# A recurrent scan on one core: first products of a chain step issued a step ahead, and small reduction products issued a step behind their operands

## The chip, the cores and the metric

One core of a Trainium2 chip runs the whole program. The metric is device time in microseconds (us). The tensor engine is called PE here, the vector engine DVE, the scalar engine ACT, GpSimd POOL, and the engine that issues most transfers SP.

## What is computed

The program is a small network over 512 latent tokens and 256 context tokens of width 1024. The change touches its first mixer alone, a linear recurrence with a 64 by 64 state per head, 16 heads, run in two directions (`wkv7_scan`), the coefficient of its bonus term, and the norm of its keys:

```python
kk = to_heads(k * k_k.astype(f32), RK_HEADS, RK_HEAD)
kk = kk / jnp.maximum(jnp.sqrt(jnp.sum(kk * kk, axis=-1, keepdims=True)), 1e-12)
...
s_kk = jnp.einsum('bhvk,bhk->bhv', s, kk_t)
s = (s * w_t[:, :, None, :] - s_kk[..., None] * (kk_t * a_t)[:, :, None, :]
     + v_t[..., None] * k_t[:, :, None, :])
return s, jnp.einsum('bhvk,bhk->bhv', s, r_t)
...
coef = jnp.einsum('bthn,zbthn,hn->bth', r, k_dir, r_k.astype(jnp.float32))
bonus = (coef[..., None] * v).reshape(b, n, D_MODEL)
```

The index z of `coef` runs over the two directions, so `coef` sums over both.

## The kernel before

The recurrence is done in chunks of 64 tokens, 12 chunks in each direction. A pair f of heads (f = 0 to 7) goes through three chains of four steps, `chain(f, 0)` to `chain(f, 2)`; the first is over the context, the other two over the latent tokens. Both directions and both heads of the pair go through a step together. A step (L844 to L896) is:

1. POOL scales the old state S (L850, tile SP). PE multiplies the values, UV, with the masked Gram matrix GA, and adds the product of S with KR to it, in place 0 of the PSUM tile `ch` (L856 and L859; for latent chunks also products into `y`, L861). ACT copies the sum out as Rs (L863). `ch` is one tile with one buffer, taken anew in each step, so the first product of a step waits until everything of the step before has been read.
2. PE multiplies Rs with the inverse TF into place 1 (L868), and ACT writes the result back into UV (L871).
3. PE multiplies UV with BT into place 2 (L877) and with GA into `y` (L881). DVE makes the new S from place 2 and SP (L890; L888 in the first step).
4. S becomes the old state of the next step; nothing is issued here.

`mm` (L831) issues all products of the chain, so the trace has them at L833; `mm` keeps the last of them in `last`. After each of the four parts the chain yields. `weave` (L991) then runs `fill` and the sides in turn. `fill` (L1030) takes as many pieces of the background work as PACE allots to this slot, 384 slots in all, and `tc.issue_after` places what they put on PE behind the last product of the chain. The background work is `job` (L954): the key, receptance and value projections of later pairs (products at L979), and behind them a conditioning product (`ada`, L235). The sides are pieces of the inversion of the next chunks (`inv`, L765: products at L790 and L795, ACT copies T at L797, DVE transposes at L799, DVE masks at L792), the Gram products (`gram`, L716, products at L739) and the features of the next pair (`feats1`, `feats2`); a side is not placed behind the chain. The order within an engine is set by a planner from the order of the code and its own estimate of when an operand is ready.

`feats2` (L667) makes, for each of the two directions in turn, the scaled keys `bk` (L693 to L701; DVE does one half of the partitions, POOL the other), and then the bonus coefficient: DVE multiplies receptance, `r_k` and this direction's keys (z, L704; the trace names the tile t), PE sums it over the head's 64 partitions with four products of two columns (L707, each in two passes, so eight records), and ACT copies the result (L709) or, for the second direction, DVE adds it (L711).

`k_out` (L327) takes a finished key projection: for each of two feature blocks ACT copies it out of PSUM (L334), SP stores it (L335), ACT squares it (L337), and PE sums the squares by products of two columns (L340). Copies and squares share the tag `st`, two buffers in the scan. `k_norm` (L343) has POOL raise the sums to the power -1/2 and PE transpose them (L348).

Of the kernel before, what the change touches and what calls it, by code (L numbers as in the profile page):

```python
# [12 lines left out]
OP = mybir.AluOpType  # L13
# [18 lines left out]
PACE = ((-13, 0), (0, 13), (28, 25), (60, 33), (76, 49), (124, 73), (140, 89), (156, 97), (172, 113),  # L32
        (220, 137), (236, 153), (252, 161), (268, 177), (384, 217))
# [271 lines left out]
def phase_rwkv(k, tables, tables2, modulate, yg):  # L305
# [18 lines left out]
    W = {"r": a["rk_w_rkv"][0, 0], "k": a["rk_w_rkv"][0, 1], "v": a["rk_w_rkv"][0, 2]}  # L324
    halves = lambda ps: ps.rearrange("p (i n) -> p i n", i=2)

    def k_out(p, pss, lat, pool, tag, psp, pt):  # L327

        c0, c1 = (0, NT) if lat else (NT, NA)
        pn = k.t(psp, [128, 512], tag=pt)[:, :24]  # L330
        for i, ps in enumerate(pss if lat else [halves(pss[0])[:, i] for i in range(2)]):
            f = 2 * p + i
            t = k.t(pool, [128, 512], tag=tag)[:, :c1 - c0]
            nc.scalar.copy(out=t, in_=ps)  # L334
            nc.sync.dma_start(out=kd_[f][:, c0:c1], in_=t)  # L335
            sq = k.t(pool, [128, 512], tag=tag)[:, :c1 - c0]
            nc.scalar.activation(out=sq, in_=ps, func=AF.Square, scale=k.v1["k_k"][:, f:f + 1])  # L337
            for b in range((c1 - c0) // 128):
                o = c0 // 32 + 4 * b + 2 * i
                nc.tensor.matmul(pn[:, o:o + 2], sq[:, b * 128:(b + 1) * 128], k.c["blk2"], start=True, stop=True)  # L340
        nc.vector.tensor_scalar(out=rq[:, c0 // 32:c1 // 32], in0=pn[:, c0 // 32:c1 // 32], scalar1=1e-24, scalar2=None, op0=OP.max)

    def k_norm(p, psp, pt):  # L343
        nc.gpsimd.tensor_tensor(out=rq, in0=rq, in1=k.mhalf.to_broadcast([128, 24]), op=OP.pow)
        for b0, b1 in ((0, 4), (4, 6)):
            ps = k.t(psp, [128, 512], tag=pt)
            for b in range(b0, b1):
                nc.tensor.transpose(ps[:4, (b - b0) * 128:(b - b0 + 1) * 128], rq[:, 4 * b:4 * b + 4], k.ident)  # L348
            hi = rn[heads(p), b0 * 128:b1 * 128]
            nc.scalar.copy(out=hi, in_=ps[:4, :(b1 - b0) * 128])  # L350
            q = 64 * (p % 2) + 32
            nc.vector.tensor_tensor(out=rn[q:q + 4, b0 * 128:b1 * 128], in0=ps[:4, :(b1 - b0) * 128], in1=hi.bitcast(F32), op=OP.subtract)

    def r_out(p, pss, lat, pool, tag, *_):
        for i, ps in enumerate(pss):
            t = k.t(pool, [128, 512], tag=tag)
            nc.scalar.copy(out=t, in_=ps)
            nc.sync.dma_start(out=rd_[2 * p + i], in_=t)

    def v_out(p, pss, lat, pool, tag, *_):  # L360
        for i, ps in enumerate(pss):
            t = k.t(pool, [128, 512], tag=tag)
            nc.vector.tensor_copy(t, ps)
            b = 2 * i if lat else 4
            nc.sync.dma_start(out=vd[b * 128:(b + 2) * 128, p * 256:(p + 1) * 256].rearrange("(b p) n -> p b n", p=128), in_=halves(t))
    OUT = {"k": k_out, "r": r_out, "v": v_out}


    with ExitStack() as ea:
# [124 lines left out]
        k_out(0, ks, True, sp3, "st", psn, "mm")  # L494
        k_out(0, [kc], False, sp3, "st", psn, "mm")
        k_norm(0, psn, "mm")
# [14 lines left out]
        for p in range(2):  # L511
            r_out(p, rs[2 * p:2 * p + 2], True, sp3, "st")
# [12 lines left out]
        v_out(0, vs[:2], True, sp3, "st")  # L525
        v_out(0, vs[2:], False, sp3, "st")


    with ExitStack() as eb:
# [137 lines left out]
        def feats2(f):  # L667
# [21 lines left out]
            for d in range(2):  # L689
# [13 lines left out]
                z = k.t(fp2, [128, NA], tag="t1")[:, :NT]  # L703
                nc.vector.scalar_tensor_tensor(out=z, in0=rT, scalar=V["r_k"][:, f:f + 1], in1=kd[:, 0:NT], op0=OP.mult, op1=OP.mult)  # L704
                ps = k.t(psf, [128, 512], tag="gm")
                for b in range(4):
                    nc.tensor.matmul(ps[:, 2 * b:2 * b + 2], z[:, b * 128:(b + 1) * 128], k.c["blk2"], start=True, stop=True)  # L707
                if d == 0:
                    nc.scalar.copy(out=cf, in_=ps[:, 0:8])  # L709
                else:  # L710
                    nc.vector.tensor_tensor(out=cf, in0=cf, in1=ps[:, 0:8], op=OP.add)  # L711
                yield
            st.update(KR=KR, BK=BK, PC=PC)
# [120 lines left out]

        def chain(f, bt):
# [8 lines left out]
            for s4 in range(4):  # L844
# [18 lines left out]
                nc.scalar.copy(out=Rs, in_=pc_[:, 0])  # L863
                yield
                for d in range(2):
                    for par in range(2):
                        q = PR(1 - par)
                        mm(pc_[q, 1, d, :], TF[q, s4, d, :], Rs[q, d, :], start=True, stop=True, skip_group_check=True)  # L868
                for par in range(2):
                    q = PR(1 - par)  # L870
                    nc.scalar.activation(out=UV[q, par, s4], in_=pc_[q, 1], func=AF.Copy, scale=-1.0)  # L871
                yield
                for d in range(2):
                    for par in range(2):
                        q = PR(par)
                        if s < 11:
                            mm(pc_[q, 2, d, :], BT[:, par, s4, d, :], UV[:, par, s4, d, :], start=True, stop=True, skip_group_check=True)  # L877
# [5 lines left out]
                if s < 11:  # L883
                    Sn = k.t(cp, [128, 2, 64], tag="S")
                    for d in range(2):
                        j = chunk_of(d, s)
                        if S is None:
                            nc.vector.tensor_scalar(out=Sn[:, d], in0=pc_[:, 2, d, :], scalar1=PC[d][:, j:j + 1], scalar2=None, op0=OP.mult)  # L888
                        else:
                            nc.vector.scalar_tensor_tensor(out=Sn[:, d], in0=pc_[:, 2, d, :], scalar=PC[d][:, j:j + 1],  # L890
# [3 lines left out]
                yield  # L894
                S = st["S"] = Sn
# [58 lines left out]
        def job(n_, p, lat):  # L954
# [55 lines left out]
        def run(g):  # L1010
            for _ in g:
                pass

# [23 lines left out]
        NG, NV, NE, F1, F2 = 3, 13, 7, 7, 9  # L1037
# [1212 lines left out]
```

## Time and profile before

| | us |
|---|---|
| median of three runs | 3043.56 |
| lowest and highest of them | 3039.95, 3060.38 |
| the profiled execution | 3043.58 |
| its span, first to last instruction | 3041.8 |
| PE busy in the span | 2665.8 (88%) |
| DVE, ACT, POOL busy | 1562.1, 1218.2, 826.3 |

A busy time is the union of an engine's instructions; PE's instructions overlap one another, and its weight loads are listed apart. An idle time in square brackets stands behind the instruction that it came before, with what ended it. The granted clock is a share of the full 2.4 GHz, and 0.5 is 1.2 GHz. The scan lies between 205 and 1080 us of the span.

### The profile page before, as it was taken

The numbers are of one execution on the slowest core, as the hardware profiler recorded it, in microseconds if no ns is written. First come the engines' busy times: TensorE is split into PE (matmuls) and PEld (weight loads), VectorE is DVE, ScalarE is ACT, GpSimd is POOL, SyncE is SP. The second block draws the span as 40 slices with busy tenths as digits, with TensorE's granted clock in tenths as the row PEclk, the third lists the DMA queues.
The fourth block names the chain that finished last, engine by engine and source line by source line (L and its number), as shares of the span: only waits on it lengthen the run. The fifth ranks groups of instructions, "written<-read, shape, count | busy, mean of one in ns | idle before, by whom it ended". The sixth has DMA issues, their size and how long they took to land. (4 is left out here: it accounts for less than half of the span.)

```text
span 3041.8 us, 49004 instructions
## 1 busy us (share of the span) xinstructions
PE 2665.8 (88%) x19592; PEld 2127.8 (70%) x19592; DVE 1562.1 (51%) x2443; ACT 1218.2 (40%) x2267; POOL 826.3 (27%) x908
## 2 busy tenths in 40 slices
PE   5878788898898766899897999999949989989999
PEld 3666677677776545677686787887837855778887
DVE  5865656756656536754446531111155467554544
ACT  5644545555555423225432321111123367342422
POOL 2453434534534321018534300000033100112120
PEclk8976788997888778999898999999979979999999
DMA  7562334544543536757622767788972212122321
GB/s 256 184 219 68 97 114 144 183 137 129 172 135 105 173 128 199 242 173 229 194 84 97 267 208 236 256 273 291 299 253 72 71 37 72 58 83 89 106 88 65
DMA packets 346594, 477.99 MB, mean 157 GB/s; under 512 B 45842, under 2 KB 242723, under 8 KB 339703
## 3 DMA queue, kind: packets, MB, share of 16 engines
q1 hardware_dynamic: 328664, 404.80, 41.2%
q0 software_dynamic: 10480, 60.31, 6.1%
q10 hardware_dynamic: 7216, 9.68, 1.0%
q8 instruction: 157, 2.57, 0.4%
q14 instruction: 77, 0.63, 0.1%
HBM read 419.34 MB, written 55.39 MB: 156 GB/s over the span
## 5 line engine op out<-in xcount | busy, mean ns | idle before, releaser
L168 DVE TENSOR_TENSOR wl<-w,wh 128x1024 fp32r<-128x1024 f32 (+1 forms) x271 | 332.1, 1232 | 473.6 <-ACT wh L167 472.4
L167 ACT CAST wh<-w 128x1024 fp32r<-128x1024 f32 (+1 forms) x271 | 256.5, 953 | 551.3 <-PE mm L173 469.3
L173 PE MATMUL mm<-act,wh 128*128 128x512 f32 x1408 | 439.6, 394 | 14.5 <-ACT act L167 14.5
L173 PEld LDWEIGHTS mm<-act,wh 128*128 128x128 f32 x1408 | 265.6, 190 | 73.7 <-ACT act L167 15.0
L173 PE MATMUL mm<-act,wl 128*128 128x512 f32 x704 | 275.5, 391 | 0.0
L173 PE MATMUL mm<-wh,act 128*128 128x512 f32 x816 | 262.0, 400 | 7.5 <-ACT wh L167 4.2
L173 PEld LDWEIGHTS mm<-wh,act 128*128 128x128 f32 x816 | 157.3, 193 | 47.0 <-ACT wh L167 7.2
L286 POOL TENSOR_TENSOR act<-act 128x512 f32<-128x512 f32 x96 | 142.7, 1491 | 139.7 <-ACT act L285 75.5
L301 POOL DMA_DIRECT2D bc<-gate x6 | 3.6, 593 | 614.4 <-DVEq L1707 523.6
L173 PE MATMUL mm<-wl,act 128*128 128x512 f32 x408 | 163.1, 400 | 2.8 <-DVE wl L168 2.8
L1220 DVE TENSOR_TENSOR silu<-silu,mm 128x512 f32<-128x512 f32 (+4 forms) x77 | 35.3, 458 | 248.3 <-PE mm L1216 183.1
L173 PEld LDWEIGHTS mm<-act,wl 128*128 128x128 f32 x704 | 133.1, 189 | 28.1
L799 DVE STREAM_TRANSPOSE XT<-T 128x512 f16<-128x512 f16 x120 | 84.6, 705 | 100.4 <-ACT T L797 100.2
L743 POOL TENSOR_TENSOR GA<-GA,masks 128x512 f32<-128x512 f32 (+1 forms) x96 | 100.1, 1053 | 103.7 <-ACT GA L742 100.5
L739 PE MATMUL gm<-kr,bk 64*128 64x128 f32 (+1 forms) x768 | 115.4, 324 | 4.2 <-ACT GA L742 2.4
L739 PEld LDWEIGHTS gm<-kr,bk 64*128 64x128 f32 x768 | 99.4, 224 | 25.2 <-ACT GA L742 9.8
L792 DVE TENSOR_TENSOR W<-pW,masks 128x512 f16<-128x512 f32 x120 | 81.9, 682 | 64.4 <-PE pW L790 63.8
L850 POOL TENSOR_TENSOR SP<-S,pc 128x64 f32<-128x64 f32 x176 | 59.2, 355 | 194.3 <-DVE S L890 183.0
L1216 PEld LDWEIGHTS mm<-moxh,w 128*128 128x128 f32 x704 | 105.0, 190 | 8.3 <-issue 5.7
L1216 PE MATMUL mm<-moxh,w 128*128 128x192 f32 (+1 forms) x704 | 108.0, 314 | 2.5 <-DMA w<-in_moe_w_dram 2.4
L797 ACT CAST T<-pT 128x512 f16<-128x512 f32 x120 | 69.7, 581 | 83.2 <-PE pT L795 79.8
L285 ACT ACTIVATE act<-act,cT 128x512 f32<-128x512 f32 x96 | 67.6, 723 | 81.6 <-DMA act<-in_w_ada_dram 81.4
(521 smaller groups left out, 6382.7 us busy)
## 6 DMA issues: line engine op xcount, KB each, us to landing
w<-in_moe_w_dram SPq DMA_DIRECT2D x109, 1024.0 KB
w<-in_ffn_w_dram SPq DMA_DIRECT2D x32, 1024.0 KB
act<-in_ada_w_dram SPq DMA_DIRECT2D x96, 256.0 KB
act<-in_w_ada_dram SPq DMA_DIRECT2D x96, 256.0 KB
w<-in_w_up_dram SPq DMA_DIRECT2D x22, 1024.0 KB
x<-xdk POOLq DMA_DIRECT2D x18, 1024.0 KB, 5.6
x<-xdv POOLq DMA_DIRECT2D x18, 1024.0 KB, 5.7
w<-in_ada_w_dram SPq DMA_DIRECT2D x32, 512.0 KB
```

The lines of the kernel that those rows point to most:

```text
L167: self.nc.scalar.copy(out=hi, in_=x)
L168: self.nc.vector.tensor_tensor(out=lo, in0=x, in1=hi.bitcast(F32), op=OP.subtract)
L173: self.nc.tensor.matmul(ps, x, y, start=start and i == 0, stop=stop and i == 2, skip_group_check=True)
L285: nc.scalar.activation(out=wt, in_=wt, func=AF.Copy, scale=c)
L286: nc.gpsimd.tensor_tensor(out=acc, in0=wt, in1=acc if kk else bias, op=OP.add)
L739: nc.tensor.matmul(pss[par][:, s2, d, :nc_], bkj(d, par, j), KR[d][PR(par), j::12, :][:, :nc_ // 64, :], start=True, stop=True)
L743: nc.gpsimd.tensor_tensor(out=out, in0=out, in1=gm, op=OP.mult)
L792: nc.vector.tensor_tensor(out=W16, in0=pW, in1=lmask[:, li, None].to_broadcast(sh), op=OP.mult)
L797: nc.scalar.copy(out=T16, in_=pT)
L799: nc.vector.transpose(fl(XT), fl(T16))
L850: nc.gpsimd.tensor_tensor(out=SP[:, d], in0=S[:, d], in1=PC[d][:, j:j + 1].to_broadcast([128, 64]), op=OP.mult)
L1216: nc.tensor.matmul(ps[:, :n], w[:, kk], xT[:, kk, :n], start=(kk == 0), stop=(kk == KB - 1))
```

## The change

The first products of a step (values with GA) leave the step. A function `ahead` issues them for the following step, after the new S of the present step has been issued and one yield later, behind the last product of the chain; it finds the next step's GA and UV across the ends of chains and pairs. `ch` becomes one tile for the whole scan with four places, of which each step takes the next three, so that the first products go into the fourth. The two directions' start flags differ: only direction 0 starts a group.

The bonus term adds the two directions' keys first and multiplies once, then yields, then has four products in place of eight and one copy. In `k_out` both copies and stores come first, then both squares, then a yield, then the products; in `k_norm` a yield stands between the power and the transposes. PACE and the count F2 of feature pieces allow for the added yields. Before the scan, the same functions are run to their end at once (`run`).

```diff
-PACE = ((-13, 0), (0, 13), (28, 25), (60, 33), (76, 49), (124, 73), (140, 89), (156, 97), (172, 113),
-        (220, 137), (236, 153), (252, 161), (268, 177), (384, 217))
+PACE = ((-13, 0), (0, 13), (28, 28), (60, 36), (76, 52), (124, 79), (140, 95), (156, 103), (172, 119),
+        (220, 146), (236, 162), (252, 170), (268, 186), (384, 227))
...
-        pn = k.t(psp, [128, 512], tag=pt)[:, :24]
-        for i, ps in enumerate(pss if lat else [halves(pss[0])[:, i] for i in range(2)]):
-            f = 2 * p + i
+        srcs = pss if lat else [halves(pss[0])[:, i] for i in range(2)]
+        for i, ps in enumerate(srcs):
             t = k.t(pool, [128, 512], tag=tag)[:, :c1 - c0]
             nc.scalar.copy(out=t, in_=ps)
-            nc.sync.dma_start(out=kd_[f][:, c0:c1], in_=t)
+            nc.sync.dma_start(out=kd_[2 * p + i][:, c0:c1], in_=t)
+        sqs = []
+        for i, ps in enumerate(srcs):
+            f = 2 * p + i
             sq = k.t(pool, [128, 512], tag=tag)[:, :c1 - c0]
             nc.scalar.activation(out=sq, in_=ps, func=AF.Square, scale=k.v1["k_k"][:, f:f + 1])
+            sqs.append(sq)
+        yield
+        pn = k.t(psp, [128, 512], tag=pt)[:, :24]
+        for i, sq in enumerate(sqs):
             for b in range((c1 - c0) // 128):
                 o = c0 // 32 + 4 * b + 2 * i
                 nc.tensor.matmul(pn[:, o:o + 2], sq[:, b * 128:(b + 1) * 128], k.c["blk2"], start=True, stop=True)
...
         nc.gpsimd.tensor_tensor(out=rq, in0=rq, in1=k.mhalf.to_broadcast([128, 24]), op=OP.pow)
+        yield
...
-                z = k.t(fp2, [128, NA], tag="t1")[:, :NT]
-                nc.vector.scalar_tensor_tensor(out=z, in0=rT, scalar=V["r_k"][:, f:f + 1], in1=kd[:, 0:NT], op0=OP.mult, op1=OP.mult)
-                ps = k.t(psf, [128, 512], tag="gm")
-                for b in range(4):
-                    nc.tensor.matmul(ps[:, 2 * b:2 * b + 2], z[:, b * 128:(b + 1) * 128], k.c["blk2"], start=True, stop=True)
-                if d == 0:
-                    nc.scalar.copy(out=cf, in_=ps[:, 0:8])
-                else:
-                    nc.vector.tensor_tensor(out=cf, in0=cf, in1=ps[:, 0:8], op=OP.add)
                 yield
+            z = k.t(fp2, [128, NA], tag="t1")[:, :NT]
+            nc.vector.tensor_tensor(out=z, in0=al[0][:, 0:NT], in1=al[1][:, 0:NT], op=OP.add)
+            nc.vector.scalar_tensor_tensor(out=z, in0=rT, scalar=V["r_k"][:, f:f + 1], in1=z, op0=OP.mult, op1=OP.mult)
+            yield
+            ps = k.t(psf, [128, 512], tag="gm")
+            for b in range(4):
+                nc.tensor.matmul(ps[:, 2 * b:2 * b + 2], z[:, b * 128:(b + 1) * 128], k.c["blk2"], start=True, stop=True)
+            nc.scalar.copy(out=cf, in_=ps[:, 0:8])
...
+        chb = k.t(psch, [128, 4, 2, 64], tag="ch")
+        place = [0]
+
+        def ahead(f, bt, s4):
+
+            if s4 == 4:
+                bt, s4 = bt + 1, 0
+            if bt == 3:
+                f, bt = f + 1, 0
+            if f == 8:
+                return
+            GA, UV = gst[f, bt]["GA"], gst[f, bt]["UV"]
+            with tc.issue_after(last[0].ins) if last[0] is not None else nullcontext():
+                for d in range(2):
+                    for par in range(2):
+                        q, uq = PR(par), PR(1 - par)
+                        mm(chb[uq, place[0] % 4, d, :], GA[q, par, s4, d, 0:64], UV[q, par, s4, d, :], start=d == 0, stop=False, skip_group_check=True)
...
-                pc_ = k.t(psch, [128, 4, 2, 64], tag="ch")
+                if s + f == 0:
+                    ahead(f, bt, s4)
+                pA, pB, pC = (chb[:, (place[0] + i) % 4] for i in range(3))
+                place[0] += 3
...
-                        mm(pc_[uq, 0, d, :], GA[q, par, s4, d, 0:64], UV[q, par, s4, d, :],
-                                         start=True, stop=S is None, skip_group_check=True)
                         if S is not None:
-                            mm(pc_[uq, 0, d, :], KR[d][q, j, 0:64], S[q, d, :], start=False, stop=True, skip_group_check=True)
+                            mm(pA[uq, d, :], KR[d][q, j, 0:64], S[q, d, :], start=False, stop=True, skip_group_check=True)
...
                 yield
+                ahead(f, bt, s4 + 1)
                 S = st["S"] = Sn
                 yield
...
-            OUT[n_](p, pss, lat, bst, "st", psg, "gm")
+            yield from OUT[n_](p, pss, lat, bst, "st", psg, "gm")
             if (n_, lat) == ("k", False):
-                k_norm(p, psg, "gm")
+                yield from k_norm(p, psg, "gm")
...
-        NG, NV, NE, F1, F2 = 3, 13, 7, 7, 9
+        NG, NV, NE, F1, F2 = 3, 13, 7, 7, 10
```

The other places of `pc_` become pA, pB and pC in the same way.

## Rows read from the trace of the kernel before

**Rows 1.** The page, first line.

```profile
span 3041.8 us, 49004 instructions
```

**Rows 2.** Stretches: length, PE, PEld, DVE, ACT, POOL busy, granted clock, DMA.

```profile
205.00:1080.00 875.00, 749.44 (x10129) 589.67 (x10129) 524.27 (x839) 454.05 (x1010) 378.59 (x542) 0.82 0.44 135
595.00:623.00 28.00, 25.04 (x211) 22.71 (x211) 15.92 (x26) 7.50 (x20) 10.20 (x15) 0.57 0.29 95
```

**Rows 3.** Waits of PE, 205 to 1080 us: total us, times, longest.

```profile
PE gm L707 <- DVE t L704: 25.4, 10, 4.1
PE ch L833 <- ACT Rs L863: 14.3, 6, 7.7
...
PE ch L833 <- DVE S L890: 7.7, 3, 2.8
...
PE y L833 <- DVE S L890: 3.9, 7, 0.9
...
PE gm L340 <- ACT st L337: 5.1, 2, 3.5
```

**Rows 4.** Sums over seven stretches of L707 alone: first direction, then second.

```profile
sum 19.10, PE 12.18; mean PE 1.74
...
sum 20.00, PE 12.10; mean PE 1.73
```

**Rows 5.** Timeline, 590 to 598 us: start, length, engine, line, operation, [idle before].

```profile
590.48 0.39 PE L979 MATMUL bg<-wh,x 128*128 128x256 f32 x1
...
591.18 0.28 PE L979 MATMUL bg<-wh,x 128*128 128x256 f32 x1
...
594.93 0.73 DVE L704 SCALAR_TENSOR_TENSOR t<-rT,tab,sgw 128x512 f32<-128x512 f32 x1
595.60 0.69 DVE L799 STREAM_TRANSPOSE XT<-T 128x512 f16<-128x512 f16 x1
...
595.72 1.87 PE L707 MATMUL gm<-ctile,t 128*128 128x2 f32 x8 [4.01 <-DVE t L704]
596.23 0.42 DVE L890 SCALAR_TENSOR_TENSOR S<-ch,pc,SP 128x64 f32<-128x64 f32 x2
...
597.52 0.49 PE L833 MATMUL ch<-UV,GA 64*64 64x64 f32 x4
```

**Rows 6.** Timelines of PE: other groups of the first direction, and what follows one.

```profile
265.74 0.48 PE L833 MATMUL ch<-UV,GA 64*64 64x64 f32 x4 [2.23 <-DVE S L890]
...
374.96 1.84 PE L707 MATMUL gm<-ctile,t 128*128 128x2 f32 x8 [1.52 <-DVE t L704]
...
817.39 1.87 PE L707 MATMUL gm<-ctile,t 128*128 128x2 f32 x8 [4.01 <-DVE t L704]
```

**Rows 7.** Timeline, 602 to 608 us, the second direction.

```profile
602.59 2.20 DVE L701 TENSOR_TENSOR bk<-sgw,cs 64x768 f32<-64x768 f32 x1
...
605.50 1.83 PE L707 MATMUL gm<-ctile,t 128*128 128x2 f32 x8 [2.03 <-DVE t L704]
...
607.26 1.12 PE L739 MATMUL gm<-kr,bk 64*128 64x64 f32 x4
```

**Rows 8.** Timelines at 188 us (first pair) and at 305 us (norm).

```profile
188.08 1.70 PE L707 MATMUL gm<-ctile,t 128*128 128x2 f32 x8
...
305.00 0.86 PE L340 MATMUL gm<-ctile,st 128*128 128x2 f32 x4 [3.54 <-ACT st L337]
```

**Rows 9.** Single lines: L699 and L863 (ns min/median/max, starts); who ended L833's idle time (us, times).

```profile
L699 DVE TENSOR_TENSOR sgw<-sgw,kT x16: 906/2324/2462, 170.2 to 933.0; 128x768 f32<-128x768 f32 x16
...
L863 ACT COPY Rs<-ch x96: 242/266/297, 210.6 to 1062.1; 128x128 f32<-128x128 f32 x96
...
  DVE S L890: 20.7, 22
```

**Rows 10.** Timeline of PE, 1049.5 to 1051 us: a step of the last pair.

```profile
1049.91 0.27 PE L833 MATMUL y<-S,kr 64*64 64x64 f32 x2
...
1050.38 0.28 PE L833 MATMUL ch<-S,kr 64*64 64x64 f32 x3
```

More of the change, by code (lines that the diff above doesn't have):

```diff
@@ L324, in phase_rwkv, with run @@
     W = {"r": a["rk_w_rkv"][0, 0], "k": a["rk_w_rkv"][0, 1], "v": a["rk_w_rkv"][0, 2]}
+    def run(g):
+        for _ in g:
+            pass
     halves = lambda ps: ps.rearrange("p (i n) -> p i n", i=2)
@@ L358, in r_out @@
             nc.sync.dma_start(out=rd_[2 * p + i], in_=t)
+        yield from ()
     def v_out(p, pss, lat, pool, tag, *_):
@@ L365, in v_out @@
             nc.sync.dma_start(out=vd[b * 128:(b + 2) * 128, p * 256:(p + 1) * 256].rearrange("(b p) n -> p b n", p=128), in_=halves(t))
+        yield from ()
     OUT = {"k": k_out, "r": r_out, "v": v_out}
@@ L493, in phase_rwkv @@
                 k.mm3(halves(lc)[:, i], w, at(x, ALL, slice(NT, NA)), kk + i == 0, kk + i == KB)
-        k_out(0, ks, True, sp3, "st", psn, "mm")
-        k_out(0, [kc], False, sp3, "st", psn, "mm")
-        k_norm(0, psn, "mm")
+        run(k_out(0, ks, True, sp3, "st", psn, "mm"))
+        run(k_out(0, [kc], False, sp3, "st", psn, "mm"))
+        run(k_norm(0, psn, "mm"))
         for i, func in enumerate((AF.Tanh, AF.Copy)):
@@ L511, in phase_rwkv @@
         for p in range(2):
-            r_out(p, rs[2 * p:2 * p + 2], True, sp3, "st")
+            run(r_out(p, rs[2 * p:2 * p + 2], True, sp3, "st"))
         wg = weights(wv_p, "r0", a["rk_g1"][0])
@@ L524, in phase_rwkv @@
                 k.mm3(halves(vs[tb // 2])[:, tb % 2], at(x, ALL, slice(tb * 128, tb * 128 + 128)), at(wv, ALL, kk), kk + tb % 2 == 0, kk + tb % 2 == KB)
-        v_out(0, vs[:2], True, sp3, "st")
-        v_out(0, vs[2:], False, sp3, "st")
+        run(v_out(0, vs[:2], True, sp3, "st"))
+        run(v_out(0, vs[2:], False, sp3, "st"))
     with ExitStack() as eb:
@@ L862, in chain @@
                 Rs = k.t(cp, [128, 2, 64], tag="Rs")
-                nc.scalar.copy(out=Rs, in_=pc_[:, 0])
+                nc.scalar.copy(out=Rs, in_=pA)
                 yield
@@ L867, in chain @@
                         q = PR(1 - par)
-                        mm(pc_[q, 1, d, :], TF[q, s4, d, :], Rs[q, d, :], start=True, stop=True, skip_group_check=True)
+                        mm(pB[q, d, :], TF[q, s4, d, :], Rs[q, d, :], start=True, stop=True, skip_group_check=True)
                 for par in range(2):
                     q = PR(1 - par)
-                    nc.scalar.activation(out=UV[q, par, s4], in_=pc_[q, 1], func=AF.Copy, scale=-1.0)
+                    nc.scalar.activation(out=UV[q, par, s4], in_=pB[q], func=AF.Copy, scale=-1.0)
                 yield
@@ L876, in chain @@
                         if s < 11:
-                            mm(pc_[q, 2, d, :], BT[:, par, s4, d, :], UV[:, par, s4, d, :], start=True, stop=True, skip_group_check=True)
+                            mm(pC[q, d, :], BT[:, par, s4, d, :], UV[:, par, s4, d, :], start=True, stop=True, skip_group_check=True)
                 if lat:
@@ L887, in chain @@
                         if S is None:
-                            nc.vector.tensor_scalar(out=Sn[:, d], in0=pc_[:, 2, d, :], scalar1=PC[d][:, j:j + 1], scalar2=None, op0=OP.mult)
+                            nc.vector.tensor_scalar(out=Sn[:, d], in0=pC[:, d, :], scalar1=PC[d][:, j:j + 1], scalar2=None, op0=OP.mult)
                         else:
-                            nc.vector.scalar_tensor_tensor(out=Sn[:, d], in0=pc_[:, 2, d, :], scalar=PC[d][:, j:j + 1],
+                            nc.vector.scalar_tensor_tensor(out=Sn[:, d], in0=pC[:, d, :], scalar=PC[d][:, j:j + 1],
                                                            in1=SP[:, d], op0=OP.mult, op1=OP.add)
@@ L1008, in weave @@
                 run(g_)
-        def run(g):
-            for _ in g:
-                pass
         def ada(row, w, b, name, c0, c1):
```

## The prediction

> **What bounds the kernel now.** The change touches one stage, the scan, so I read the views in this order: the span, the busy time by stretch, the waits of PE, the matmul groups that the change edits, and the order of time around two of them. The profiled execution took 3043.58 us, of which the span is 3041.8 [rows 1]; the median of the three runs is 3043.56, so the sum below can be made against either. From 205 to 1080 us the scan fills PE for 749.4 of 875 us [rows 2]: PE is the bound, and 125.6 us of idle time plus a mean granted clock of 0.82 is all that a better order can win. The chain is stretched by that work: its 96 steps take 8.9 us each (Rs from 210.6 to 1062.1 [rows 9]), and S and Rs together end few of PE's idle times, as follows.
>
> Who ends PE's idle time [rows 3]: the bonus products L707 waiting for their operand z (named t, L704), 25.4 us in ten waits, is the longest entry by far. The state S (L890) ends 11.6 us (7.7 and 3.9), Rs 14.3 (7.7 of it one wait at the very end), and the norm products L340 wait 5.1 us for their square. So the change aims at some 42 us of the 125.6.
>
> The second thing to see is the clock. Seven times the features of the next pair are made (L667 to L714). In the stretch around one of them, 595 to 623 us, PE is busy for 25 of 28 us but at a granted clock of 0.57, that is mostly at 1.2 and not 2.4 GHz [rows 2], and a group of eight two-column passes takes 1.87 us [rows 5].
>
> The third is who makes z late. In [rows 5] the vector engine starts L704 at 594.93, as L701 ends, with no gap; PE sits idle 4.01 us; and S is evicted only at 596.23, because it stands in the same queue behind L704 and L799. L699 takes 0.906 to 2.462 us, median 2.324 [rows 9]: the long ones run beside GpSimd's half of the same work. The Trainium skill, SBUF — State Buffer, section Who interferes with whom, says that a VectorE operation with two SBUF inputs contends with GpSimd for the shared port; the spread of L699 agrees, and by it the delay stays, whatever PE does.
>
> **Bonus products, first direction.** Today each pair has two groups of four products (eight passes); the change adds the two directions first and leaves one. Seven groups go from the scan, 12.2 us of PE time [rows 4]. Three of them also ended a wait: 1.52 and 4.01 us at the first and last of the three [rows 6], and 4.01 in [rows 5], 9.5 us together. Most that can come back: 21.7 us. But a wait for z becomes one for S. In [rows 5], without L704 and L707, S follows L701 (end about 595.0) and L799 (0.69): its 0.42 us end at 596.1, and the products of L833 start near 596.2 in place of 597.52, so 1.3 us, not 5.9. After the first group, at 262 us, PE waits another 2.23 us for S [rows 6], so nothing comes back there. I take 1.3 twice, 1.8 for the group with the short wait, 1.85 for each of the three that no wait stands ahead of or behind, and 0 for the first: **-10**; ends -5.6 and -21.7.
>
> **Second direction.** The group stays (seven of them, 12.1 us [rows 4]) but moves behind a yield. It holds 15.9 us of the waits (25.4 less 9.5). What is late next is the Gram products L739, which need L701 alone: in [rows 7] L701 ends at 604.79, so they could start some 2.4 us before 607.26. The group must still be done later: 1.83 us at the low clock, half at the full one, so 0.6 to 1.5 us of the 2.4 remain. VectorE pays an add of some 0.73 us (taken as L704) once and saves one L704 and a small add: nothing net. I take 1.0 per pair: **-7**; ends 0 and -15.9. The first pair, made before the scan, has its second group right ahead of L739 and it lasts 1.70 us [rows 8]: **-1.6**.
>
> **Norm products.** L340 waits 5.1 us in all [rows 3]; 3.54 of it in [rows 8], where the square (L337) is late; squares and copies share two buffers, and a buffer comes free when its copy is stored. The change makes both copies first, then both squares, and yields. The squares then wait for the stores of both copies, once for both since the stores follow each other; ScalarE's stall stays, and PE's goes into background products of the next piece. What is queued behind the square on ScalarE is Rs and UV of the chain. The transposes behind GpSimd's power get the same step. I take **-4**; ends 0 and -5.1.
>
> **First products a step ahead.** Nothing is removed: 96 times eight passes move from just ahead of the S products to behind the eviction of S's predecessor, one slot of background work earlier. On PE's time that is nothing, hidden by PE being full. On the chain, the 24 passes from 1049.91 to 1050.66 [rows 10] become 16, so 0.25 us a step. That counts only where little else is queued, in the 12 steps of the last pair: at best -3. Whether the products can run before S is evicted, no row shows: today the one buffer of the tile holds them back until then. The bank is still one tile, and the eviction of S reads it. If they wait for S, every background piece of the next slot is put behind them by `issue_after`, and loses its use as cover for S. Such a piece lasts 0.98 us (590.48 to 591.46 [rows 5]), about every second slot has one (199 in 356 by PACE), and today S ends 22 idle times of PE and its loads [rows 9]: 22 x 0.5 x 0.98 = +11. I take **+2**, nearer the gain, since independent work of the inversion is not put behind them; ends -3 and +11. The Trainium skill, PSUM — Partial Sum Buffer, section PSUM bank collisions raise a hardware error, says that TensorE may not write a bank and quadrant while VectorE reads any column of it; by it rival 4 holds. No run here shows it.
>
> **Clock.** A mean of 0.57 is 86% of the 28 us at half speed, (1 - 0.57) / 0.5. At full speed that work would give back half, 12 us a pair, 84 in all; at the other end nothing, since S still leaves PE idle in the same places. Nearer to the second: **-5**.
>
> **Pacing.** PACE and the slot counts give the added yields their own slots, so the background work keeps its rate: 0. The tail may shift by the 7.7 us that one Rs waits behind weight splits; I keep that for the range.
>
> Sum: -10 - 7 - 1.6 - 4 + 2 - 5 = -25.6, and 3043.6 - 25.6 = **3018**.
>
> **Rivals.** 1. *The waits are handed to S.* For it: VectorE is full through [rows 5], and the 2.23 us behind the first group. Against: three groups have no wait at either side. Then -5.6 - 1.6 - 2 and +5 remain: 3043.6 - 4 = 3039. 2. *The clock comes back.* The low stretch in [rows 2] begins where the 4.01 us of idle time in [rows 5] end, and holds two of the two-column groups. Against: L739 and the chain's products stay there. With half of the 84 us, 42 in place of 5: 2981. 3. *Slower: the background held behind the first products.* PE blocks on S at the products, in slots that a piece covers now. With a piece lost in half of all 96 steps, 96 x 0.5 x 0.98 = 47 in place of 2: 3063. It decides from 28 lost pieces on (27.6 / 0.98). Against: S ends only 22 waits now. 4. *The rotating places free nothing:* the products wait for the eviction that reads their bank. For it: in [rows 5] they start after S today, but there one buffer alone accounts for that. It gives +11 in place of +2 where the cover is lost, 3027, and 3016 where all is covered; both lie in the forecast's case, and I give it 0.3 of that case's 0.55.
>
> **Chances.** Forecast, a gain of 12 to 45 us: 0.55 (rival 4 within it). Handed on, within 12 us: 0.18. Clock, over 45 us: 0.17. Slower by over 12 us: 0.10. One per cent is 30.4 us, about what a measurement of this kernel tells from no change. Above that gain lie 0.20 of the forecast's 0.55 and the clock's 0.17: faster 0.37. Slower by over 30.4 us is 0.06, the rest 0.57. The range, 2978 to 3050, leaves out some 0.06 below (the clock's far end) and 0.08 above. The forecast's own range is 2999 to 3032.
>
> **What would show it.** In the changed kernel: PE's waits of the bonus products under 5 us and half their passes; S ending more idle time than 11.6 us, by up to 10 us; L739 following L701 within 0.3 us; the wait of the norm products near 0; the first products of a step starting after S's eviction ends and not before; the scan's granted clock at 0.82 to 0.84; the last Rs near 1035. I am wrong if S's share grows by over 20 us (rivals 1 and 3), if the low stretches halve (rival 2), or if a transfer, not the scan's end, sets when the next phase starts.

## The result: 0.9% slower, and the profile after

| | before | after |
|---|---|---|
| median of the runs side by side, us | 3041.24 | 3069.66 |
| ratio, 95% interval | | 1.0090 [1.0072, 1.0108] |
| the profiled execution | 3043.58 | 3061.77 |
| first Rs to last Rs | 210.6 to 1062.1 | 201.6 to 1091.9 |
| bonus passes of PE, records | 128 | 64 |

The change costs 27 us. I forecast a gain of 26; the time lies above my whole range.

The first line of the changed kernel's page:

```profile
span 3060.0 us, 48863 instructions
```

Its scan, first Rs to last, and the stretch of [rows 2] (columns as there):

```profile
202.00:1092.00 890.00, 758.18 (x10045) 592.52 (x10044) 526.23 (x820) 448.44 (x997) 385.32 (x537) 0.81 0.42 129
595.00:623.00 28.00, 20.92 (x228) 18.70 (x228) 17.04 (x21) 6.86 (x18) 12.33 (x13) 0.63 0.28 90
```

The kernel before, the same stretch from its own first Rs to its last:

```profile
211.00:1062.00 851.00, 737.94 (x10060) 581.29 (x10060) 513.73 (x826) 443.06 (x992) 371.24 (x534) 0.83 0.43 131
```

The scan is 39 us longer. PE's idle time grew from 113.1 to 131.8 us, and its busy time grew too, by 20 us, with no more to do (10045 records of PE in place of 10060): the mean granted clock fell from 0.83 to 0.81. Counting work done at the lower level at half its time, PE did 614.6 us of full-speed work before and 610.2 after; 247 us of its busy time lay at the lower level before, 297 after. So 39 is +19 of idle time, +25 of clock, -4 of work. The scan began 9 us earlier and ended 30 us later, about what the medians differ by. Behind it 12 us came back bit by bit, in stages that the change leaves alone (matching products start 24 us later near 1800 us and 18 at the end, where the span grew by 18.2); whether that is more than the scatter of single executions is not shown.

Waits of PE in the changed kernel, 205 to 1100 us (columns as in [rows 3]):

```profile
PE pT L806 <- DVE W L803: 20.4, 16, 4.1
PE ch L844 <- DVE S L921: 14.8, 7, 4.5
PE y L844 <- DVE S L921: 9.5, 8, 5.8
...
PE gm L722 <- DVE t L718: 7.6, 4, 4.6
...
PE gm L349 <- ACT st L342: 7.4, 3, 4.1
...
PE ch L844 <- ACT Rs L894: 6.0, 7, 1.8
```

Against [rows 3] the bonus products' wait fell from 25.4 to 7.6 us, as the edit meant. S ends 24.3 in place of 11.6 us. The inversion's products pT waiting for their masked operand W now lead the list with 20.4. The norm products wait more, not less: 7.4 against 5.1. The line of W in the kernel before:

```profile
PE pT L795 <- DVE W L792: 5.0, 7, 2.2
```

The place of [rows 7], the second direction's keys of the same pair, in the changed kernel (columns as in [rows 5]):

```profile
601.06 0.49 PEld L801 LDWEIGHTS <-nl 128*128 128x128 f16 x8
...
601.45 0.95 DVE L713 TENSOR_TENSOR bk<-sgw,cs 64x768 f32<-64x768 f32 x1
...
602.32 0.68 DVE L168 TENSOR_TENSOR wl<-w,wh 128x512 fp32r<-128x512 f32 x1
602.93 2.28 DVE L717 TENSOR_TENSOR t<-sgw,sgw 128x512 f32<-128x512 f32 x1
605.14 0.27 DVE L921 SCALAR_TENSOR_TENSOR S<-ch,pc,SP 128x64 f32<-128x64 f32 x1
605.33 0.69 DVE L810 STREAM_TRANSPOSE XT<-T 128x512 f16<-128x512 f16 x1
...
605.96 0.23 DVE L921 SCALAR_TENSOR_TENSOR S<-ch,pc,SP 128x64 f32<-128x64 f32 x1
...
606.24 0.69 PE L844 MATMUL ch<-UV,GA 64*64 64x64 f32 x8 [4.53 <-DVE S L921]
```

This is rival 1: DVE is full from 601.45 on, S waits in its queue behind the new add of the two directions (L717, 2.28 us) and PE, which waited 2.03 us for z here before, waits 4.53 us for S. The instruction that waits is the first product of the next step. At the place of [rows 5], the first direction, the 4.01 us for z have become 0.98 us for S:

```profile
594.37 0.45 PE L844 MATMUL ch<-UV,GA 64*64 64x64 f32 x8 [0.98 <-DVE S L919]
```

The other first-direction place with a wait of 4.01 us, 817.39 in [rows 6], shows the hand-over best where the bonus alone is changed (e2 below). There S stands behind three instructions of DVE, and PE waits 5.29 us for it:

```profile
816.43 2.55 DVE L701 TENSOR_TENSOR bk<-sgw,cs 64x768 f32<-64x768 f32 x1
818.90 0.94 DVE L693 SCALAR_TENSOR_TENSOR t<-sgw,kk 128x768 f32<-128x768 f32 x1
819.77 0.69 DVE L798 STREAM_TRANSPOSE XT<-T 128x512 f16<-128x512 f16 x1
...
820.40 0.42 DVE L889 SCALAR_TENSOR_TENSOR S<-ch,pc,SP 128x64 f32<-128x64 f32 x2
...
820.97 0.49 PE L832 MATMUL ch<-UV,GA 64*64 64x64 f32 x4 [5.29 <-DVE S L889]
```

In the changed kernel the bonus group of pair 5, made during pair 4, still waits for its own operand:

```profile
735.76 2.55 DVE L713 TENSOR_TENSOR bk<-sgw,cs 64x768 f32<-64x768 f32 x1
738.24 1.63 DVE L717 TENSOR_TENSOR t<-sgw,sgw 128x512 f32<-128x512 f32 x1
739.90 0.75 DVE L718 SCALAR_TENSOR_TENSOR t<-rT,tab,t 128x512 f32<-128x512 f32 x1
...
740.71 1.87 PE L722 MATMUL gm<-ctile,t 128*128 128x2 f32 x8 [4.56 <-DVE t L718]
...
742.50 1.97 PE L750 MATMUL gm<-kr,bk 64*128 64x64 f32 x8
```

It waits longer than the second direction's group of that pair did before (0.97 us, at 719.74), and what follows this wait is the clock at its lower level (same kernel, by stretch):

```profile
739.80:763.70 23.90, 22.99 (x198) 19.70 (x199) 9.09 (x18) 7.44 (x19) 4.81 (x12) 0.50 0.21 68
```

PE is busy for 22.99 of 23.90 us, all at 1.2 GHz. Counted at full speed that is half.

### The profile page after: what moved, and what is told of

It is laid out like the page before. It is cut to its first block, busy times and chain, and to the rows that moved or that the text cites. A ratio compares the mean times of both kernels' runs of the same rounds, so it can differ in the third digit from the quotient of the medians.

```text
span 3060.0 us, 48863 instructions
## 1 busy us (share of the span) xinstructions
PE 2666.1 (87%) x19528; PEld 2125.5 (69%) x19528; DVE 1565.9 (51%) x2435; ACT 1220.6 (40%) x2267; POOL 838.0 (27%) x908
## 5 line engine op out<-in xcount | busy, mean ns | idle before, releaser
L880 POOL TENSOR_TENSOR SP<-S,pc 128x64 f32<-128x64 f32 x176 | 66.6, 396 | 220.5 <-DVE S L921 213.5
```

What stands on the lines that cost most here:

```text
L880: nc.gpsimd.tensor_tensor(out=SP[:, d], in0=S[:, d], in1=PC[d][:, j:j + 1].to_broadcast([128, 64]), op=OP.mult)
```

## The experiments

Six theories were tried. A: the background pinned behind the early first products (rival 3). B: the norm part, split into B1, the order inside `k_out`, and B2, the added background steps with the new PACE. C: the bonus. D: the order of the next pair's inversion against the chain at the pair boundaries. E: denser background between the chain's steps, or the waits in `k_out`. F: the shift of the background steps against the chain. All ratios stand against the kernel before run on the same chip (medians there 3033 to 3041); 0.001 is 3 us. Where two kernels stand in a row the interval is that of the second. "Idle" is PE's between first and last Rs, "low" PE's busy time there at the lower clock level, both worked out from the profiled execution, one for each kernel. Two profiles of one kernel (e8 and e12, e11 and e16) differ by up to 12 us of scan and 24 us of low time; a smaller difference between two single profiles says little. The scan begins anywhere from 198 to 212 us, so a longer scan is not a later end by as much.

| kernel | holds | ratio, 95% interval | scan | idle | low |
|---|---|---|---|---|---|
| before | | 1 | 851 | 113 | 247 |
| after | ahead, bonus, order, steps | 1.0090 [1.0072, 1.0108] | 890 | 132 | 297 |
| e1 | ahead | 0.9985 [0.9963, 1.0007] | 857 | 109 | 257 |
| e2 | bonus | 1.0015 [0.9996, 1.0035] | 864 | 126 | 273 |
| e3 | order, steps | 1.0047 [1.0022, 1.0072] | 883 | 124 | 301 |
| e4 | bonus, order, steps | 1.0052 [1.0029, 1.0074] | 876 | 125 | 289 |
| e5 | order | 1.0049 [1.0021, 1.0077] | 881 | 116 | 300 |
| e6 | steps | 1.0055 [1.0029, 1.0081] | 865 | 122 | 276 |
| e7 | ahead, bonus, steps | 1.0059 [1.0036, 1.0081] | 874 | 132 | 272 |
| e8, e12 | ahead, bonus | 0.9978, 0.9970 [0.9953, 0.9987] | 845, 833 | 114, 111 | 241, 217 |
| e9 | late inversion alone | 1.0054 [1.0036, 1.0071] | 873 | 121 | 289 |
| e10 | after, inversion early | 1.0100 [1.0075, 1.0124] | 882 | 125 | 291 |
| e11, e16 | e8, inversion early | 0.9931, 0.9926 [0.9906, 0.9947] | 833, 840 | 116, 120 | 213, 224 |
| e13 | ahead, bonus, order, no steps | 0.9973 [0.9954, 0.9991] | 853 | 109 | 268 |
| e14 | new PACE alone | 1.0027 [1.0007, 1.0047] | 869 | 121 | 281 |
| e15 | e13, inversion early | 0.9980 [0.9961, 0.9999] | 854 | 114 | 255 |

**The parts one by one.** e1_only_ahead has `ahead` and the four places alone; e2_only_bonus the bonus with F2 = 10; e3_only_norm the order in `k_out`, the yields and the new PACE; e4_no_ahead is the changed kernel with the chain of before.

```diff
@@ e1, chain @@
+        chb = k.t(psch, [128, 4, 2, 64], tag="ch")
...
+                ahead(f, bt, s4 + 1)
@@ e2, feats2 @@
+            nc.vector.tensor_tensor(out=z, in0=al[0][:, 0:NT], in1=al[1][:, 0:NT], op=OP.add)
...
+            yield
@@ e3, k_out, k_norm, PACE @@
+        yield
...
+PACE = ((-13, 0), (0, 13), (28, 28), (60, 36), (76, 52), (124, 79), (140, 95), (156, 103), (172, 119),
...
```

> The kernel before with the first products a step ahead and nothing else (pacing, bonus and norm products as before). Theory A, the background of the fourth slot is held behind products that wait for S: the whole loss of the changed kernel and more, 30 to 50 us slower than before, and background pieces between the first products and the S products in about half of the steps. Theory B, the loss comes from the pacing and the added yields: within 10 us of before. Theory C, the loss comes from the bonus products: within 10 us of before.

> The kernel before with the bonus term alone changed (and its one added feature piece). Theory A: 10 to 25 us faster than before, as the prediction's terms for the bonus products say. Theory B: 0 to 25 us faster, since the pacing is that of before. Theory C, the wait for z becomes a wait of the inversion and of S and the clock falls more often: 15 us or more slower.

> The kernel before with the norm products a step later, the added yields of the key jobs and the new pacing. Theory A: 0 to 5 us faster. Theory B: 15 us or more slower. Theory C: 0 to 5 us faster.

> The changed kernel without the first products a step ahead (bonus and norm products and the pacing stay). Theory A: 10 to 30 us faster than before. Theory B: 15 us or more slower than before, about as the changed kernel. Theory C: 15 us or more slower than before.

Measured, e1 to e4: 0.9985, 1.0015, 1.0047, 1.0052. A and C fall: neither part loses by itself beyond its interval. The norm part costs 14 us where I had a gain of 4. The rest of the 27 appears only when the parts stand together.

**The norm part taken apart.** e5_copies_first has both copies before both squares, no added step, the old PACE. e6_empty_steps has the yields and the new PACE and `k_out` in its old order. e7_no_reorder is the changed kernel with `k_out` in its old order. e8_ahead_bonus is the changed kernel without the norm part.

```diff
@@ e5, k_out @@
+        srcs = pss if lat else [halves(pss[0])[:, i] for i in range(2)]
+        for i, ps in enumerate(srcs):
...
+        sqs = []
+        for i, ps in enumerate(srcs):
...
+        for i, sq in enumerate(sqs):
@@ e6, the end of k_out, and k_norm behind the power @@
+        yield
...
+        yield
@@ e7, against the changed kernel, k_out @@
-        yield
-        pn = k.t(psp, [128, 512], tag=pt)[:, :24]
-        for i, sq in enumerate(sqs):
...
+        yield
```

> The kernel before with only the order inside k_out changed: both copies and their stores, then both squares, then all norm products, no added step and the pacing table of before. Theory B1 (the loss of the norm part sits in this order: the first square now waits on ScalarE for the store of a copy, as in e3_only_norm, where that wait summed to 15.2 us against 8.7 and 7.5 in e1_only_ahead and before): 3045 to 3055. Theory B2 (the loss sits in the pacing: more background steps per chain slot, and empty ones among them): within 5 us of before, 3035 to 3043.

> The kernel before with the pacing table of after and the added steps, but k_out's work in its old order: the step behind k_out issues nothing, the one in k_norm stands between the power and its transposes. B1: 3036 to 3042, as before. B2: 3046 to 3055, the same as e3_only_norm (3053), with the scan's last Rs as late as there.

> The changed kernel with k_out's work in its old order (bonus, first products a step ahead, added steps and new pacing stay). B1: 3040 to 3050, most of the 27 us comes back. B2: 3060 to 3070, nothing comes back. If the part that appears only in combination (after against e4_no_ahead, some 11 us) rests on the order in k_out, it lies between.

> The kernel before with the first products a step ahead and the bonus products moved, norm part and pacing table as before. If the parts add up (e1_only_ahead -2, e2_only_bonus +2): 3035 to 3042. If the first products ahead cost the 11 us as soon as the background between the steps is shifted, whatever shifts it: 3045 to 3052. The pair boundaries (TF of step 0 behind its Rs) tell it: with the loss, three or more pairs stand over 9 us, without it one or two.

Measured, e5 to e8: 1.0049, 1.0055, 1.0059, 0.9978. B1 and B2 each hold alone and do not add up: order and steps together (e3) cost no more than either. e7 still loses, so the order cannot be the main carrier in the changed kernel (0.0031, some 9 us, came back); e8, without the norm part, does not lose at all. The reason that B1 gave, squares that wait for a store, does not hold: in e5 they wait 5.2 us so, in before 7.5. In e5's profile PE's idle time hardly grew (113 to 116); nearly all by which its scan is longer is low clock.

**The pair boundaries.** In the profiles a pattern went with the loss: at the boundaries to pairs 3 and 5 the sixteen products pT of the inversion's fifth level stood on PE behind TF times Rs of step 11 in e3 to e7 and in the changed kernel, ahead of it in before, e1 and e8, and behind it at one of the two in e2. e9_late_start delays that inversion in the kernel before; e10_early_start issues its first piece early in the changed kernel (`inv(f, 2)` and this piece are then paced together, as 14 pieces in place of 13); e11_early_no_shift does so without the norm part; e12_ahead_bonus_again repeats e8.

```diff
@@ e9, beside chain(f, 2) @@
-sides = [(inv(f + 1, 0), NV), ...
+sides = [(seq(iter([None] * (f in (2, 4))), inv(f + 1, 0)), NV + (f in (2, 4))), ...
@@ e10 and e11, beside chain(f, 1); iv goes on beside chain(f, 2) @@
-sides = [(inv(f, 2), NV)]
+iv = inv(f + 1, 0) if nx else None
+sides = [(seq(inv(f, 2), (next(iv) for _ in range(1))), NV + 1)]
```

> The kernel before, nothing of the change in it; only the inversion for the first batch of pairs 3 and 5 begins one piece later. In TensorE's order the sixteen products of its fifth level then stand behind step 11's TF times Rs at exactly these two boundaries (in before they stand ahead of it there, in every kernel that lost 14 us and more they stand behind it at both). Theory D (the order of the inversion against the chain at the pair boundaries carries the loss): the stretch from step 11's Rs to step 1's Rs grows from 15.8 and 16.1 us to 21 to 25 at pairs 3 and 5, and the time by 10 to 18 us, as in e3_only_norm, e5_copies_first and e6_empty_steps. Theory E (denser background between the chain's steps, or the waits in k_out, carry it): within 4 us of before.

> The changed kernel, all its parts kept; only the first piece of the inversion for a pair's first batch is issued at the end of the batch before, one piece earlier. In TensorE's order the fifth level's products then stand ahead of step 11's TF times Rs at all pairs (in the changed kernel they stand behind it at pairs 2, 3 and 5). D: the stretches of pairs 2, 3 and 5 fall from 21.5, 24.7 and 21.7 us to 15 to 19, and the time by 13 to 27 us, to 3042 to 3056 beside a before of 3041. E: 3064 to 3074, as the changed kernel.

> The control for e10_early_start: first products ahead and bonus moved (e8_ahead_bonus, whose boundary order is that of before but at pair 1), with the same early start of the inversion. D: little to win where the order was right already: within 6 us of e8_ahead_bonus in this call. If the early start is a gain of its own whatever the order, it is 13 us or more below it, and e10_early_start proves nothing.

> The same kernel as e8_ahead_bonus, in more rounds: the parts of the change that move no background step. D: faster than before by 3 to 12 us (ratio 0.996 to 0.999). If its first look was chance: 1.000 or more.

Timeline of PE at the boundary to pair 3 (start, length, engine, line, operation), before:

```profile
573.58 0.44 PE L795 MATMUL pT<-W,XT 64*64 64x64 f16 x16
573.85 0.42 PE L833 MATMUL ch<-Rs,TF 64*64 64x64 f32 x8
...
582.37 0.45 PE L833 MATMUL ch<-Rs,TF 64*64 64x64 f32 x8
```

and with the late start, e9:

```profile
575.11 0.42 PE L833 MATMUL ch<-Rs,TF 64*64 64x64 f32 x8
...
579.88 0.44 PE L795 MATMUL pT<-W,XT 64*64 64x64 f16 x16
...
584.34 0.66 PE L750 MATMUL gm<-ctile,bk 128*128 128x128 f32 x4 [1.60 <-ACT GA L742]
...
589.19 0.41 PE L790 MATMUL pW<-T,nl 128*128 128x64 f16 x8 [2.73 <-DVE T L783]
...
591.89 0.69 PE L833 MATMUL ch<-Rs,TF 64*64 64x64 f32 x8
```

From one TF times Rs to the next it is 8.5 us before and 16.8 us in e9: the last level of the inversion falls behind step 11, other work is queued ahead of its end, and the chain waits. From the end of step 11's Rs to the start of step 1's Rs the two boundaries grew from 15.8 and 16.1 to 30.0 and 25.5 us, more than expected, and the kernel lost 16 us. So a late inversion is enough for a loss of the size of e3. It is not what the changed kernel loses by: in e10 the seven boundaries sum to 122 us in place of 139 (pair 3: 15.6, down from 24.7), and the time stayed, 1.0100. Pairs 2, 4 and 5 took 126, 124 and 116 us there, about as long as in the changed kernel. D falls as the explanation and stands as a mechanism; e13 below has the late order at both boundaries (25.6 and 21.7 us) and loses nothing. e11, my control, was not neutral: the early start gained another 12 us on e12, so what it does depends on the rest of the order.

**The steps in the changed kernel.** e13_norm_no_steps keeps all parts, but puts the squares into the step of the job's last projection products and the norm products into the next one, so that no step is added and PACE is that of before. e14_pace_alone has only the new PACE. e15_no_steps_early and e16_early_again add the early start to e13, and repeat e11.

```diff
@@ e13, against the changed kernel: job, then k_norm, then PACE as before @@
-                    if i % 2 == 1 or (lat and n_ != "v"):
+                    if (i % 2 == 1 or (lat and n_ != "v")) and not (n_ == "k" and kk == KB - 1 and o is acc[-1]):
                         yield m
...
-        yield
...
+PACE = ((-13, 0), (0, 13), (28, 25), (60, 33), (76, 49), (124, 73), (140, 89), (156, 97), (172, 113),
...
```

> The changed kernel with all three parts, but the norm part without added steps: the squares go out in the step of the job's last projection products, the norm products in the next one, the transposes right behind the power, and the pacing table is that of before. Theory F (the shift of the background steps carries the norm part's loss): 3020 to 3040 beside a before of 3035, near e8_ahead_bonus (ratio 0.994 to 1.002). Theory B1 (k_out's order, the squares waiting on ScalarE for a store, carries it): 3044 to 3058. Its order at the boundaries of pairs 3 and 5 has the inversion late, so theory D wants 3040 to 3055 too.

> The kernel before with the pacing table of the changed kernel and nothing else: the same background steps, denser by 3 in 24 in the stretches with the projections of k, and done earlier. F, if density is what hurts: 3044 to 3056, with longer stretches at the lower clock level in pairs 2 and 4. If the steps' places against the chain decide and not the density, or if earlier is simply earlier: 3028 to 3042. The inversion is ahead at the boundaries of pairs 2 to 6, so theory D wants no loss there.

> e13_norm_no_steps with the early start of the inversion of e10_early_start. Late boundaries left: pairs 2 and 7 in place of 3 and 5. If early start pays wherever the background is unshifted (e11_early_no_shift, ratio 0.993): 3010 to 3032. If it pays only with k_out as before: 3040 and more.

> The same kernel as e11_early_no_shift, in more rounds: first products ahead, bonus moved, inversion begun a piece early, norm part and pacing of before. If its 0.9931 was real: 0.990 to 0.996, some 12 to 30 us faster than before; if it was drift of one look: 0.997, as e12_ahead_bonus_again.

Measured, e13 to e16: 0.9973, 1.0027, 0.9980, 0.9926. This places the loss: the changed kernel without its added steps and table is 36 us faster (0.0117) than with them, and as fast as e8. The other runs agree: the six kernels with the steps and the table (after, e3, e4, e6, e7, e10) all lose 14 us or more. Of those without, only e5 and e9 lose as much, by other changes of the order. e13 too has an order of its own, so it shows that the other parts need not lose, and not by which wait the steps do. Pairs 2 to 5 by stretch (columns as in [rows 2]), the changed kernel first, then e13:

```profile
453.70:576.40 122.70, 108.47 (x1261) 84.69 (x1260) 70.66 (x109) 63.82 (x142) 50.38 (x68) 0.82 0.42 131
576.40:700.30 123.90, 104.80 (x1321) 82.12 (x1320) 80.33 (x113) 59.31 (x134) 60.00 (x82) 0.81 0.45 136
700.30:824.10 123.80, 108.62 (x1244) 86.62 (x1243) 68.29 (x103) 62.01 (x136) 51.02 (x67) 0.77 0.42 130
824.10:941.30 117.20, 98.75 (x1352) 77.24 (x1352) 73.23 (x109) 57.78 (x129) 51.86 (x71) 0.82 0.42 127
```

```profile
455.00:560.10 105.10, 97.77 (x1260) 77.29 (x1259) 66.84 (x105) 62.06 (x137) 51.89 (x67) 0.87 0.49 155
560.10:675.40 115.30, 99.95 (x1303) 79.54 (x1303) 76.49 (x112) 58.75 (x133) 57.19 (x78) 0.84 0.47 143
675.40:789.80 114.40, 104.55 (x1254) 82.19 (x1255) 67.19 (x104) 61.88 (x138) 53.05 (x67) 0.79 0.45 143
789.80:901.90 112.10, 100.32 (x1356) 79.56 (x1354) 72.17 (x106) 57.05 (x129) 53.06 (x68) 0.81 0.43 133
```

The four pairs take 487.6 against 446.9 us, 40.7 more; the other four, together, 3 less. Over the scan the 37.5 us of difference are 23.3 of idle time and half of 28.4 us more at the lower level, with the same 610 us of full-speed work. The wait that shrank most is the first one of the list above; in e13 the waits read:

```profile
PE ch L843 <- DVE S L920: 13.7, 11, 4.2
PE pT L805 <- DVE W L802: 10.4, 12, 3.2
...
PE y L843 <- DVE S L920: 3.1, 6, 0.9
```

against 14.8, 20.4 and 9.5. The wait for W is not the loss by itself: in e15 W ends 27.7 us, and e15 is as fast as e13. e14 puts the denser table alone at 8 us [2, 14] (its runs spread from 3025 to 3050); by difference, if the two add up, the steps in it cost the rest of e6's 17. The best kernel is e11 and e16: first products ahead, bonus moved, inversion a piece early, norm part and PACE as before, 0.9926, some 22 us faster than before and 50 faster than the change.

What stays open: why e5, the order alone, loses 15 us on the kernel before and nothing in e13; why the early start pays in e11 and not in e10 or e15; and whether the lower clock level is the cause of the lost time or only goes with the idle time. A kernel with work put into the waits could tell the last; no run has that.

## Why the prediction was wrong, step by step

**Pacing, 0: the step that failed.** I argued that PACE gives the added steps slots of their own and so keeps the rate. It does, nearly: the change adds nine steps, three for each of three key projections, and the table ten slots. The rate was not the point. The added steps move every projection piece behind them against the chain, the features and the inversion, and the planner then orders all engines anew. Steps and table cost +17 us alone (e6) and +36 in the company of the other parts (the changed kernel against e13); through which wait is not shown. No rival named it; the nearest, rival 3, priced the background pinned behind `ahead`, and `ahead` alone is -5 us with an interval across zero (e1).

**Bonus, first direction, -10, and second, -7.** e2 measures +5 us [-1, +11] for the whole bonus part. The passes that left were worth less than their time: of seven first-direction groups six ran at the lower clock level, and the 12.2 us of [rows 4] are 6.6 at full speed. The waits for z fell from 25.4 to 5.4. Both came back in e2's profile as 12.9 us more idle time and 25 us more at the lower level (half of it, 12.6; the 25 is no more than two profiles of one kernel differ by). Between first and last Rs, S ends 20.3 us of PE's idle time in place of 12.2, UV 17.6 in place of 8.8, W 12.2 in place of 5.1. Rival 1 (waits handed to S, and here to UV and W too) is what happened; I had it at 0.18. The second term had a fault of its own: in all eight pairs the Gram products still stand behind the bonus group on PE, as in the rows at 740.71 and 742.50, since the next pair's Gram comes after its features in the code. From the end of `bk` to the Gram it is 3.68 us on average after and 2.94 before, not 0.3. And the add that I took at 0.73 us as L704 is longer:

```profile
L717 DVE TENSOR_TENSOR t<-sgw,sgw x8: 674/1200/2284, 182.6 to 969.0; 128x512 f32<-128x512 f32 x8
```

(ns, shortest, median, longest, then starts.) At 602.93 it runs 2.28 us beside POOL's half of `bk`, which lasts 3.17. The Trainium skill, SBUF — State Buffer, section Who interferes with whom, has this contention of a VectorE operation with two SBUF inputs; I cited it for L699 and did not apply it to the instruction that the change adds. The trace agrees in the main: the add takes 2.28 us in the three places where it overlaps that half for 1.74 us and 0.67 us with GpSimd idle, but also 0.68 us at 847.83, beside that half throughout.

**First pair, -1.6.** Its group too still stands right ahead of the Gram products (186.32 and 188.09), so the yield gained nothing here. That the scan began 9.0 us earlier is not this term: e5 and e14, which leave the bonus alone, begin at 201.1 and 202.1, and e12, which has it, at 208.5.

**Norm products, -4.** In the order without steps nothing is left of it: e13 and e8 are equal within their intervals, and their wait is 6.3 us in e13, 7.4 in the changed kernel, 5.1 before. The square is what is late: ACT waits 11.7 us in five squares for a store to free one of the two buffers, 7.5 us in three before. That is not the new order's doing: e12, with the old order, has 11.7 us too, and before the squares also waited 5.9 us for a buffer that norm products still read. A step between square and product does not help a square that waits for a store.

**First products, +2, ends -3 and +11: no miss that the noise would show.** e1 gives -5 [-11, +2]. With other parts beside it the same edit is worth -14 (e12 against e2) or +12 (the changed kernel against e4), so it has no price of its own. Rival 4 holds in each profile: of 88 steps whose first product follows an eviction of S, none starts before that eviction ends, though its place in the bank is free and its operands are old. In the changed kernel 31 start within 0.2 us of its end, 22 before. Three such waits sum to 12.2 us of the 14.8 in the list, the one at 606.24 among them. The Trainium skill, PSUM — Partial Sum Buffer, section PSUM bank collisions raise a hardware error, says that they may not run beside it. The runs agree in so far as they wait, and none shows an overlap; but what the products wait for is a semaphore that S's instruction raises, so the order is the program's, and no run shows what the chip would do without it.

**Clock, -5: wrong sign.** 50 us more busy time at the lower level, so +25. In 595 to 623 us the clock did rise, 0.57 to 0.63, but PE was idle 7 us in place of 3. Here, removing PE work at a place where DVE sets the pace made idle time. In e8 and e12 the term has my sign, with 241 and 217 us at the lower level, -3 and -15 us; in e13, with 268, it has not.

**Signs.** Bonus waits under 5: 7.6. S up to 10 more than 11.6: 12.7 more. Norm near 0: 7.4. Clock 0.82 to 0.84: 0.81. Last Rs near 1035: 1091.9 (1041.1 in e12, 1036 in e11). The first products of a step did start after S's eviction, as forecast. Of my signs of being wrong the first two did not come, since S's share grew by less than 20 us and the low stretches grew; they would not have told me of this loss. The parts that move no background step come out at -9 us (e12), where the same terms summed to -21.6.

## What to carry to other kernels

Where a list of background pieces is woven into a full chain, a yield is an edit of its own: it moves everything behind it. Put the late operand and its product into steps that exist (e13) before adding one, and time an empty step by itself (e6). When PE stops waiting for one operand of DVE, look in DVE's queue for the next one: in e2 a wait of 4.01 us for z became one of 5.29 us for S in the same place, and in the changed kernel one of 2.03 us became one of 4.53, behind the instruction that the change added.

## What the runs showed that was not expected

Kernels with nearly the same work, between 602 and 620 us at full speed, spread from 833 to 890 us of scan, in the main by order: idle time by 24 us (109 to 132) and busy time at the lower clock level by 88 us (213 to 301), which is 44. The count at full speed is itself no finer than some 10 us: it is 605.3 in e6 and 614.9 in e5, which have the same products. The low level is the larger share, and it moves without the idle time: e5 has 3 us more idle time than before and 52 us more at the lower level. One fall comes in a long wait of PE: 4.56 us idle, then 23.9 us at 0.50 with PE busy for 22.99 of them. The low stretch around the wait of 4.53 us, in contrast, begins ahead of that wait, behind 10.20 us at full clock in which PE was busy for 5.59 between short waits (changed kernel, columns as in [rows 2]):

```profile
589.60:599.80 10.20, 5.59 (x102) 4.50 (x102) 10.17 (x11) 5.30 (x12) 9.81 (x7) 1.00 0.13 44
599.90:601.70 1.80, 1.80 (x14) 1.56 (x13) 1.76 (x2) 0.12 (x1) 0.91 (x2) 0.50 0.00 0
```
